# Two buffers of their own for the second weight quarter of a seven-product MLP round

## The chip, the cores and the metric

The kernel runs on one core of one Trainium2 chip. The metric is the time of one execution on the device in microseconds (us). TensorE (PE) multiplies, VectorE (DVE) and ScalarE (ACT) work on tiles, GpSimd (POOL) does small work and issues some transfers, and SyncE (SP) issues nearly all loads. A profile is one execution recorded by the hardware profiler. Its own time is its span, from the first to the last instruction.

## The reference, cut to what matters

Two token mixers (latent attention, then a Mamba-2 block) alternate with two dense MLPs, on 256 tokens of width 2048 in float32. The change lies in the MLP, which runs twice, with weights of 2048 x 8192 and 8192 x 2048:

```
def rms_norm(x, g):
    xf = x.astype(jnp.float32)
    y = xf * lax.rsqrt(jnp.mean(xf * xf, axis=-1, keepdims=True) + RMS_EPS)
    return (y * g.astype(jnp.float32)).astype(x.dtype)

def squared_relu_mlp(h, w_in, w_out):
    u = jax.nn.relu(h @ w_in)
    return (u * u) @ w_out

    for i in range(DEPTH):
        ...
        x = x + mix
        h = rms_norm(x, mlp_norm_g[i])
        x = x + squared_relu_mlp(h, mlp_w_in[i], mlp_w_out[i])
```

## The kernel before

**The stream of units.** All weights come as units of 128 x 1024 float32 (512 KB): two blocks of 128 rows of the contraction by 512 columns. `Flow` holds the list of units in the order in which PE uses them. Each unit is loaded by SP (line 85), then cut into a high and a low part so that three matmuls in PE's fast float32 format give nearly the full product: ACT writes the rounded high part `wh` (line 102), DVE subtracts it and writes the low part `wl` (line 103). The pools `wh` and `wl` have four buffers each. The pool of raw weights, `raw`, has six. The number in a tile's name is the number of its unit: `wl245` is the low part of unit 245.

**A round of seven products.** The first product of the MLP, 256 tokens by 2048 by 8192, runs in eight rounds p of 1024 hidden columns. Round 0 is computed in the plain way. Rounds 1 to 7 cut the tokens, the contraction and the columns into halves and use seven products of half-size blocks (M1, N7, N5, N6, N4, M2, N3) where eight would be needed. Each product runs in four steps d = 0 to 3 of two row blocks (six matmuls, lines 616 to 618). For a step four quarters of the weights are wanted: the first (b11) in pool `rx`, the second (b12), the fourth (b22), and the third for M2. DVE forms the combinations at line 183, in place:

```
if name == "N7":
    add("b22", "b12", "b22")
...
if name == "N5" and d not in LATE5:
    add("b12", "b11", "b12")
...
if name == "N6":
    add("b11", "b11", "b22")
    ...
"N7": lambda: [load("b12", B12, (0, 1)), load("b22", "raw", (1, 1))],
```

So the buffer of b12 is held from its load until the low part of N5 has been made from it, and the buffer of b22 from its load until the sum for N6 has read it. `LATE5` is empty.

**What sets the order.** `plan()` writes the order of PE's units by hand: products of round p are mixed with units `o` of the second product (w_out, `mo`) of the round before. PE's order is kept as written. The orders on SP, DVE, ACT and POOL are chosen when the program is built, by a scheduler that places each instruction where its own estimate sees it ready, so a new pool moves rows on these engines. On each engine the instructions run strictly in that order: SP holds back all loads behind one that still waits for a buffer.

**Units named below.** In the first MLP, round p = 4 has N7 of steps 0 to 3 as units 228, 234, 242 and 251; N6 of step 0 is unit 231, and units 246 and 247 belong to w_out. In round p = 7, N7 of steps 1 to 3 are units 368, 376 and 384.

Of the kernel before, what the change touches and what calls it, by code (L numbers as in the profile page):

```python
# [169 lines left out]
def seven(layer, p, src):  # L170
# [9 lines left out]
    def unit(flow, name, d):  # L180
# [22 lines left out]
        def load(k, pool, q):  # L203
            st[k] = Load(pool, quarter(d, *q))
            return st[k]

        loads = {"M1": lambda: [load("b11", "rx", (0, 0))],
                 "N7": lambda: [load("b12", B12, (0, 1)), load("b22", "raw", (1, 1))],
                 "M2": lambda: [load("M2", "raw", (1, 0))], "N3": lambda: [load("N3", "raw", (1, 1))]}
# [5 lines left out]
class Trunk:  # L215
# [294 lines left out]
    def mlp(self, layer, gain):  # L510
        with ExitStack() as ctx:
            mp = ctx.enter_context(self.tc.tile_pool(name="mlp", bufs=1, reuse_waits="tile"))
            for name, n in (("rx", 4), ("ry", 1)):
                self.flow.pools[name] = ctx.enter_context(self.tc.tile_pool(name=name, bufs=n, reuse_waits="tile"))
            self.flow.ahead = (4, 3)
            self.mlp_body(mp, layer, gain)
# [881 lines left out]
             "x7", "z5", "z6", "o2a", "z7", "o2b", "o3"]  # L1398


B12 = "raw"
WARM = 9
LATE5 = ()
TR = (10, 8, 7, 7, 5)
# [66 lines left out]
def sequence(d):  # L1471
# [23 lines left out]
    def mlp(i):  # L1495
# [9 lines left out]
        for nb in range(4):  # L1505
            for q in range(2):
                add(("mo", i, 7, nb, q), mo[14 + q, nb])

    mlp(0)
    col = lambda name, i: {"z": 0, "x": 8, "B": 16, "C": 18}[name] + i  # L1510
    si = lambda name, i: [add(("si", name, i, q), d["si"][q, col(name, i)]) for q in range(4)]
    so = lambda k, nb: add(("so", k, nb), d["so"][k, nb])
    for step in SSM_ORDER:
# [8 lines left out]
        else:  # L1522
            for pair in ((0, 1), (2, 3)):
                for k in (6, 7):
                    for nb in pair:
                        so(k, nb)
    mlp(1)
    return seq

# [78 lines left out]
```

## Time and profile before

| what | value |
|---|---|
| median of 3 runs (lowest to highest) | 2285.51 us (2285.43 to 2286.36) |
| span of the profiled execution | 2284.5 us |
| first MLP, about 271 to 925 us: PE, DVE, ACT busy | 653.83, 586.18, 414.11 us of 654.00 |
| second MLP, about 1606 to 2284.5 us: PE, DVE, ACT busy | 675.21, 594.88, 417.07 us of 678.50 |
| DMA moved in all | 557.16 MB, mean 244 GB/s |

The profiled execution has its span of 2284.5 us; the median of the timed runs lies 1.0 us above it. A matmul's end is modelled in the trace, so the distance from one matmul's start to the next tells of a wait, not its length. The rows of a timeline give the start, the duration, the engine, the line, the operation, what is written and read, and how many equal instructions are merged (x3: the duration runs from the first start to the last end).

### The profile page before, as it was taken

Reading aid. Unit: us, or ns where it says so; the run is one execution under the profiler, and the core shown is the slowest. Engines: PE = TensorE matmul, PEld = TensorE weight load, DVE = VectorE, ACT = ScalarE, POOL = GpSimd, SP = SyncE. Lnnn points to the kernel's source line nnn. Section 1 sums busy time; section 2 is a strip of 40 time slices with the busy share of each in tenths; the row PEclk is TensorE's granted clock in tenths of the full one; section 3 lists DMA queues with packets and bytes.
Section 4 is the critical chain, followed back from the end, with each engine's and each line's share of the span. In section 5 each row is a group of like instructions: output and inputs, shape, how many; then the busy total and the mean of one; then the engine's idle time right before and its main releaser. Section 6 shows DMA issues by size and latency. Waiting matters only on the chain.

```text
span 2284.5 us, 30768 instructions
## 1 busy us (share of the span) xinstructions
PE 2278.1 (100%) x10929; PEld 1889.6 (83%) x10929; DVE 1915.9 (84%) x2318; ACT 1390.1 (61%) x1947; POOL 275.5 (12%) x315
## 2 busy tenths in 40 slices
PE   9999999999999999999999999999999999999999
PEld 7898888888888888888888888888888888888887
DVE  7786698999898897687899688676989889989985
ACT  7775576566666666564666555545666666666663
POOL 1440000000000000100133213121000000000000
PEclk9999999999999999999999999999999999999999
DMA  8545678888888878667888787767688888888874
GB/s 315 173 153 159 211 230 267 259 255 270 264 255 259 267 232 271 227 208 241 277 280 278 245 275 264 229 222 229 204 265 248 259 270 253 260 275 247 267 232 160
DMA packets 167706, 557.16 MB, mean 244 GB/s; under 512 B 19040, under 2 KB 28192, under 8 KB 166528
## 3 DMA queue, kind: packets, MB, share of 16 engines
q1 hardware_dynamic: 151264, 502.44, 66.2%
q0 software_dynamic: 13888, 48.49, 10.0%
q10 hardware_dynamic: 2400, 4.27, 0.5%
q8 instruction: 86, 1.41, 0.3%
q14 instruction: 68, 0.56, 0.1%
HBM read 529.65 MB, written 6.41 MB: 235 GB/s over the span
## 4 chain that ended last, share of the span: by engine, by line
PE 96%; DVE 1%; DMA 1%; ACT 1%; issue 1%; POOL 0%; SPq 0%; ACTq 0%; DVEq 0%
PE acc L339 13%; PE acc L340 13%; PE acc L343 13%; PE yp L618 9%; PE yp L617 9%; PE yp L616 9%; PE st L617 7%; PE st L618 7%; PE st L616 7%; DMA wraw<-mi 1%; PE sm L324 1%; DVE wl L103 1%; PE y L1309 1%; PE sm L322 1%; PE acc L616 1%; PE acc L618 1%
## 5 line engine op out<-in xcount | busy, mean ns | idle before, releaser
L102 ACT ACTIVATE wh<-wraw 128x1024 fp32r<-128x1024 f32 (+1 forms) x818 | 856.2, 1053 | 570.4 <-PE acc L340 268.9
L103 DVE TENSOR_TENSOR wl<-wraw,wh 128x1024 fp32r<-128x1024 f32 (+1 forms) x818 | 985.5, 1221 | 240.6 <-ACT wh L102 216.6
L616 PE MATMUL yp<-wh,k 128*128 128x512 f32 x896 | 349.2, 390 | 0.0
L618 PE MATMUL yp<-wh,k 128*128 128x512 f32 x896 | 348.8, 389 | 0.0
L617 PE MATMUL yp<-wl,k 128*128 128x512 f32 x896 | 348.6, 389 | 0.0
L339 PE MATMUL acc<-wh,xt 128*128 128x512 f32 x704 | 279.7, 397 | 0.4 <-ACT wh L102 0.4
L340 PE MATMUL acc<-wh,xt 128*128 128x512 f32 x704 | 274.9, 390 | 0.1
L102 ACT ACTIVATE wh<-wrx 128x1024 fp32r<-128x1024 f32 x168 | 177.8, 1058 | 153.4 <-PE yp L618 101.7
L103 DVE TENSOR_TENSOR wl<-wrx,wh 128x1024 fp32r<-128x1024 f32 x168 | 204.3, 1221 | 36.6 <-ACT wh L102 35.6
L618 PEld LDWEIGHTS yp<-wh,k 128*128 128x128 f32 x896 | 168.2, 188 | 35.1
L617 PEld LDWEIGHTS yp<-wl,k 128*128 128x128 f32 x896 | 168.2, 188 | 34.9
L616 PEld LDWEIGHTS yp<-wh,k 128*128 128x128 f32 x896 | 168.2, 188 | 34.8
L339 PE MATMUL acc<-wh,k 128*128 128x512 f32 x496 | 196.5, 396 | 0.0
L340 PE MATMUL acc<-wh,k 128*128 128x512 f32 x496 | 193.3, 390 | 0.0
L343 PE MATMUL acc<-wl,xt 128*128 128x512 f32 x704 | 188.3, 389 | 0.0
L616 PE MATMUL st<-wh,xt 128*128 128x512 f32 x448 | 177.7, 397 | 0.0
L618 PE MATMUL st<-wh,xt 128*128 128x512 f32 x448 | 174.9, 390 | 0.0
L617 PE MATMUL st<-wl,xt 128*128 128x512 f32 x448 | 174.7, 390 | 0.0
L339 PEld LDWEIGHTS acc<-wh,xt 128*128 128x128 f32 x704 | 132.7, 188 | 29.4 <-ACT wh L102 1.6
L340 PEld LDWEIGHTS acc<-wh,xt 128*128 128x128 f32 x704 | 132.5, 188 | 28.5 <-issue 1.2
L343 PEld LDWEIGHTS acc<-wl,xt 128*128 128x128 f32 x704 | 132.1, 188 | 27.7
L199 POOL DMA_DIRECT2D wrx<-mi x56 | 49.2, 878 | 720.6 <-DVE wl L103 524.5
(318 smaller groups left out, 3527.0 us busy)
## 6 DMA issues: line engine op xcount, KB each, us to landing
wraw<-mi SPq DMA_DIRECT2D x256, 512.0 KB, 5.5
wraw<-mo SPq DMA_DIRECT2D x256, 512.0 KB, 5.6
wraw<-si SPq DMA_DIRECT2D x160, 512.0 KB, 5.2
wraw<-so SPq DMA_DIRECT2D x64, 512.0 KB, 5.2
wrx<-mi SPq DMA_DIRECT2D x56, 512.0 KB, 5.4
wrx<-mi POOLq DMA_DIRECT2D x56, 512.0 KB, 7.8
wraw<-wo SPq DMA_DIRECT2D x32, 512.0 KB, 4.0
taps<-xD SPq DMA_DIRECT2D x16, 768.0 KB, 8.4
```

What stands on the lines that cost most here:

```text
L102: self.last = nc.scalar.activation(h[:, v], raw[:, v], AF.Copy)
L103: self.last_lo = nc.vector.tensor_tensor(lo[:, v], raw[:, v], h[:, v].bitcast(F32), ALU.subtract)
L199: nc.gpsimd.dma_start(st["b11"].tile, quarter(d, 1, 0), accum_op=ALU.add)
L322: self.nc.tensor.transpose(b.bitcast(F32R)[:, v], words[:, v], self.ident_r)
L324: self.nc.tensor.transpose(b[:, v], src[:, v], self.ident)
L339: nc.tensor.matmul(accs[t][:, :n], ah, wh[:, q, :], start=first and kt + q == 0, stop=False)
L340: nc.tensor.matmul(accs[t][:, :n], al, wh[:, q, :], start=False, stop=False)
L343: nc.tensor.matmul(accs[t][:, :n], lhs(kt + q, t)[0], wl[:, q, :], start=False, stop=en and q == nk - 1)
L616: nc.tensor.matmul(b, ah, wh, start=first and q == 0, stop=False)
L617: nc.tensor.matmul(b, ah, wl, start=False, stop=False)
L618: nc.tensor.matmul(b, al, wh, start=False, stop=last and q == 1)
L1309: nc.tensor.matmul(y[t][c, o], part(t)[:, c], xg[g][t][:, o], start=True, stop=True)
```

## The change

```
-            for name, n in (("rx", 4), ("ry", 1)):
+            for name, n in (("rx", 4), ("ry", 1), ("rb", 2)):
                 self.flow.pools[name] = ctx.enter_context(self.tc.tile_pool(name=name, bufs=n, reuse_waits="tile"))
...
-B12 = "raw"
+B12 = "rb"
```

The MLP opens a pool `rb` of two buffers of 128 x 1024, and every second quarter (b12) of a round is loaded into it. The six `raw` buffers are left to the other weights. Each of 28 b12 loads per MLP moves the same bytes as before. PE's rows are the same and in the same order; rows on SP and DVE change place. Three places follow, with the buffer numbers kept; the last number in a name only tells tiles apart.

SP, at the start of round p = 4 of the first MLP, before (unit 224 ends round 3; 225, 226, 229, 232 and 235 belong to w_out; 228 and 234 are N7 of steps 0 and 1, each with two loads, b12 and b22):

```order
L85 DMA wraw224_5370<-mi0 128x1024
L85 DMA wrx250_5799<-mi0 128x1024
L85 DMA wraw225_5389<-mo0 128x1024
L85 DMA wraw226_5409<-mo0 128x1024
L85 DMA wraw228_5446<-mi0 128x1024
L85 DMA wraw228_5448<-mi0 128x1024
L85 DMA wraw229_5460<-mo0 128x1024
L85 DMA wraw232_5506<-mo0 128x1024
L85 DMA wraw234_5546<-mi0 128x1024
L85 DMA wraw234_5548<-mi0 128x1024
L85 DMA wraw235_5562<-mo0 128x1024
```

and now:

```order
L85 DMA wraw224_5373<-mi0 128x1024
L85 DMA wrx250_5802<-mi0 128x1024
L85 DMA wraw225_5392<-mo0 128x1024
L85 DMA wraw226_5412<-mo0 128x1024
L85 DMA wraw228_5451<-mi0 128x1024
L85 DMA wraw229_5463<-mo0 128x1024
L85 DMA wraw232_5509<-mo0 128x1024
L85 DMA wraw234_5551<-mi0 128x1024
L85 DMA wraw235_5565<-mo0 128x1024
```

The two b12 loads are gone from here (they stand many rows earlier as `wrb`). The b22 load of unit 234 now takes over the buffer of unit 224, where it took that of unit 226.

DVE, in the middle of the same round, before (`wraw251` are the two quarters of N7, step 3; x00 and x10 are the residual sums that free the two PSUM banks of pool `yp`):

```order
L103 TENSOR_TENSOR wl241_5715<-wrx241_5662,wh241_5714 128x1024
L183 TENSOR_TENSOR wrx241_5662<-wrx241_5662,wraw242_5682 128x1024
L103 TENSOR_TENSOR wl242_5733<-wraw242_5682,wh242_5732 128x1024
L103 TENSOR_TENSOR wl243_5745<-wraw243_5700,wh243_5744 128x1024
L103 TENSOR_TENSOR wl244_5758<-wraw242_5680,wh244_5757 128x1024
L103 TENSOR_TENSOR wl245_5771<-wrx241_5662,wh245_5770 128x1024
L103 TENSOR_TENSOR wl246_5782<-wraw246_5742,wh246_5781 128x1024
L436 TENSOR_TENSOR x00_142<-yp_544_5660,x00_142 128x512
L436 TENSOR_TENSOR x10_146<-yp_545_5661,x10_146 128x512
L183 TENSOR_TENSOR wraw251_5813<-wraw251_5811,wraw251_5813 128x1024
L103 TENSOR_TENSOR wl247_5802<-wraw247_5754,wh247_5801 128x1024
```

and now:

```order
L103 TENSOR_TENSOR wl241_5718<-wrx241_5665,wh241_5717 128x1024
L183 TENSOR_TENSOR wraw251_5816<-wrb251_5814,wraw251_5816 128x1024
L103 TENSOR_TENSOR wl242_5736<-wraw242_5685,wh242_5735 128x1024
L103 TENSOR_TENSOR wl243_5748<-wraw243_5703,wh243_5747 128x1024
L183 TENSOR_TENSOR wrx241_5665<-wrx241_5665,wraw242_5685 128x1024
L103 TENSOR_TENSOR wl244_5761<-wrb242_5683,wh244_5760 128x1024
L183 TENSOR_TENSOR wrb251_5814<-wrx250_5802,wrb251_5814 128x1024
L103 TENSOR_TENSOR wl245_5774<-wrx241_5665,wh245_5773 128x1024
L103 TENSOR_TENSOR wl246_5785<-wraw246_5745,wh246_5784 128x1024
L436 TENSOR_TENSOR x00_142<-yp_544_5663,x00_142 128x512
L436 TENSOR_TENSOR x10_146<-yp_545_5664,x10_146 128x512
L103 TENSOR_TENSOR wl247_5805<-wraw247_5757,wh247_5804 128x1024
```

The two sums of step 3 (line 183, unit 251) have moved ahead of the low parts of units 242 and 245 and of the residual sums. The same move is made in rounds 3 to 6 of both MLPs.

DVE, in the last round p = 7 of the first MLP, before:

```order
L103 TENSOR_TENSOR wl370_7792<-wraw368_7707,wh370_7791 128x1024
L103 TENSOR_TENSOR wl371_7810<-wraw371_7759,wh371_7809 128x1024
L183 TENSOR_TENSOR wraw376_7839<-wraw376_7837,wraw376_7839 128x1024
L103 TENSOR_TENSOR wl372_7822<-wrx359_7555,wh372_7821 128x1024
L183 TENSOR_TENSOR wraw376_7837<-wrx375_7819,wraw376_7837 128x1024
L103 TENSOR_TENSOR wl373_7843<-wrx365_7653,wh373_7842 128x1024
L103 TENSOR_TENSOR wl374_7856<-wraw374_7807,wh374_7855 128x1024
L436 TENSOR_TENSOR x00_142<-yp_637_7772,x00_142 128x512
L436 TENSOR_TENSOR x10_146<-yp_638_7773,x10_146 128x512
```

and now:

```order
L103 TENSOR_TENSOR wl370_7795<-wrb368_7710,wh370_7794 128x1024
L183 TENSOR_TENSOR wraw376_7842<-wrb376_7840,wraw376_7842 128x1024
L103 TENSOR_TENSOR wl371_7813<-wraw371_7762,wh371_7812 128x1024
L183 TENSOR_TENSOR wrb376_7840<-wrx375_7822,wrb376_7840 128x1024
L103 TENSOR_TENSOR wl372_7825<-wrx359_7558,wh372_7824 128x1024
L103 TENSOR_TENSOR wl373_7846<-wrx365_7656,wh373_7845 128x1024
L183 TENSOR_TENSOR wraw384_7961<-wrb384_7959,wraw384_7961 128x1024
L103 TENSOR_TENSOR wl374_7859<-wraw374_7810,wh374_7858 128x1024
L436 TENSOR_TENSOR x00_142<-yp_637_7775,x00_142 128x512
L436 TENSOR_TENSOR x10_146<-yp_638_7776,x10_146 128x512
```

Here too a sum of step 3 (unit 384) now stands ahead of the low part of unit 374 and of the residual sums, and the sum of step 2 (unit 376) ahead of the low part of unit 371.

## The prediction, made before the change was run

> **What bounds the kernel now.** I read the page's busy times first, then the waits by engine, then the stalls one by one in the timelines.
>
> ```profile
> PE 2278.1 (100%) x10929; PEld 1889.6 (83%) x10929; DVE 1915.9 (84%) x2318; ACT 1390.1 (61%) x1947; POOL 275.5 (12%) x315
> 271.00:925.00 654.00, 653.83 (x2961) 539.63 (x2959) 586.18 (x579) 414.11 (x452) 40.76 (x58) 1.00 0.83 256
> PE yp L939 <- ACT xt L944: 0.5, 1, 0.5
> PEld st L617 <- DVE wl L103: 3.2, 8, 0.5
> DVE wraw L183 <- DMA wraw<-mi: 18.1, 27, 2.0
> ```
>
> The second row is the stretch of the first MLP (length, then PE, PEld, DVE, ACT, POOL busy, clock, DMA share, GB/s): PE is busy in 653.83 of 654.00 us at the full granted clock. DVE is 90% busy behind it, so it has little to give. The largest wait of PE itself that is not at the kernel's start is 0.5 us, in attention. Of the weight loads ahead of PE, one wait belongs to the seven-product rounds: eight times, 3.2 us in all, for a low part from DVE. DVE's own wait for quarters (18.1 us) is far larger, but it costs only what reaches PE. So PE bounds the kernel, and a change in loads can give back little. That is the first thing to hold against any large gain.
>
> Where one of the eight waits comes from (round 4 of the first MLP, times from the span's start; DVE, then SP, then PE):
>
> ```profile
> 553.13 3.49 DVE L103 TENSOR_TENSOR wl<-wraw,wh 128x1024 fp32r<-128x1024 f32 x3
> 563.45 1.23 DVE L183 TENSOR_TENSOR wraw<-wraw,wraw 128x1024 f32<-128x1024 f32 x1 [0.54 <-DMA wraw<-mi]
> 566.33 1.22 DVE L183 TENSOR_TENSOR wrx<-wrx,wraw 128x1024 f32<-128x1024 f32 x1
> 568.73 1.23 DVE L103 TENSOR_TENSOR wl<-wrx,wh 128x1024 fp32r<-128x1024 f32 x1
> 555.51 1.47 SPq L85 DMA_DIRECT2D wraw<-mi  x2
> 569.55 0.40 PE L616 MATMUL st<-wh,sN 128*128 128x512 f32 x1
> 570.01 0.50 PE L617 MATMUL st<-wl,sN 128*128 128x512 f32 x1
> 570.35 0.40 PE L618 MATMUL st<-wh,sN 128*128 128x512 f32 x1
> 570.58 0.39 PE L616 MATMUL st<-wh,sN 128*128 128x512 f32 x1
> ```
>
> At 563.45 DVE stands 0.54 us for the quarters of unit 234 (N7, step 1). The sum for N6 of step 0 (566.33) and its low part (568.73) queue behind it, and PE, which wants that low part, starts its second matmul 0.46 us after the first and its third 0.34 us after that, where the step is 0.23 (570.35 to 570.58). That is 0.23 + 0.11 = 0.34 us lost. The two loads of unit 234 left SP only at 555.51 and 556.65, when the low parts of units 225 and 226 (second and third of the row at 553.13) had freed two of the six buffers.
>
> **The change part by part.** Counts do not change: as many loads, sums, splits and matmuls as before, so there is no work to add or take off. Only times of arrival move.
>
> (a) The stall above goes. The b12 load of unit 234 leaves this queue, and the b22 load takes the buffer of unit 224, freed when the first of the three low parts ends, at 553.13 + 1.22 = 554.35, instead of going out at 556.65. That is 2.3 us earlier for a wait of 0.54 us; the wait ends, unless `rb` itself is late. It is not: its buffer is released by the low part of N5 two steps back, more than 20 us before. Eight waits of 3.2 us in all, at the shown rate of 0.34 us of PE for a wait of 0.5: 3.2 x 0.34 / 0.5 = 2.2 us gained. Bounds: 0 and 3.2.
>
> The Trainium skill, Perfetto Trace Analysis, section Optimization Strategy, says that the same gap repeating on the engine that should be saturated can mean too little SBUF for the next tile, in the number of buffers. This trace agrees, with eight gaps of the same kind; by that rule alone the sum would be (a), and nothing would come back.
>
> (b) What is late next: the sums of step 3. In rounds 3 to 6 they now stand ahead of low parts that PE is about to want. The rows of before, DVE first, then the load queue, then PE:
>
> ```profile
> 584.88 2.35 DVE L103 TENSOR_TENSOR wl<-wrx,wh 128x1024 fp32r<-128x1024 f32 x2
> 588.41 3.49 DVE L103 TENSOR_TENSOR wl<-wraw,wh 128x1024 fp32r<-128x1024 f32 x3
> 594.50 1.28 DVE L436 TENSOR_TENSOR x<-yp,x 128x512 f32<-128x512 f32 x2
> 597.31 1.23 DVE L183 TENSOR_TENSOR wraw<-wraw,wraw 128x1024 f32<-128x1024 f32 x1 [1.53 <-DMA wraw<-mi]
> 578.09 3.70 SPq L85 DMA_DIRECT2D wraw<-mo  x4
> L183 DVE TENSOR_TENSOR wrx<-wrx,wraw x1: 1218/1218/1218, 580.2 to 580.2; 128x1024 f32<-128x1024 f32 x1
> DMA to landing us min/median/max: 4.3/6.4/6.6
> 590.92 0.39 PE L617 MATMUL st<-wl,sN 128*128 128x512 f32 x1
> 596.37 0.39 PE L617 MATMUL st<-wl,sN 128*128 128x512 f32 x1
> 597.50 0.39 PE L616 MATMUL yp<-wh,k 128*128 128x512 f32 x1
> ```
>
> The landing row is of the four loads that left from 578.09 on. The b22 of unit 251 now takes the buffer that the N6 sum of step 1 frees (580.2 + 1.22 = 581.4; 580.9 in the change, since DVE lost 0.54 us ahead of it). With the median landing of 6.4 us it is there at 587.3. DVE reaches the sum at 587.24 - 0.5 = 586.7 (end of the row at 584.88), stands 0.6 us, and starts it at 587.3. From there DVE is full, one operation per 1.135 us ((3.49 - 1.22) / 2): low part of 242 from 588.4 to 589.7, of 243 to 590.8, a sum, the low part of 244, another sum, the low part of 245 from 594.1 to 595.3, of 246 to 596.5, then the residual sums, the first until 597.1. PE, itself 0.34 us earlier, wants 242 at 590.6, 245 at 596.0 and, at 597.2, the bank that the first residual sum frees. So all is in time, by 0.1 us at the tightest place. At the longest landing of the four, 6.6, PE loses 0.1 us. At 4.3 there is a margin of 2.2. I take 0.1 us a round in 2 x 4 rounds, +0.8 us. Bounds: 0, and with 7.3 us, the longest landing of this pool near this place
>
> ```profile
> DMA to landing us min/median/max: 3.6/5.4/7.3
> ```
>
> (the loads from 552 to 572 us), 0.8 us a round, +6.4 us.
>
> (c) The last round. The sum of unit 384 stands ahead of the low part of 374 and the residual sums:
>
> ```profile
> 830.86 1.22 DVE L103 TENSOR_TENSOR wl<-wraw,wh 128x1024 fp32r<-128x1024 f32 x1
> 834.51 1.23 DVE L183 TENSOR_TENSOR wraw<-wraw,wraw 128x1024 f32<-128x1024 f32 x1 [0.81 <-DMA wraw<-mi]
> 839.06 1.22 DVE L103 TENSOR_TENSOR wl<-wraw,wh 128x1024 fp32r<-128x1024 f32 x1
> 840.19 1.28 DVE L436 TENSOR_TENSOR x<-yp,x 128x512 f32<-128x512 f32 x2
> DMA to landing us min/median/max: 4.5/6.7/7.0
> 842.01 0.39 PE L616 MATMUL yp<-wh,k 128*128 128x512 f32 x1
> ```
>
> After the low part of 370 (until 832.1) DVE now makes the sum of 376, whose wait of 0.81 us goes, and then the low part of 371, until 834.4; that frees the buffer for the b22 of 384. The four loads from 829.8 to 833.7 us took 4.5 to 7.0. From the sum's start it is 1.14 + 1.14 + 0.68 = 2.95 us to the end of the first residual sum, which PE wants at 842.0; the sum may start at 839.05 at the latest, so a landing up to 4.65 us costs nothing, and the median of 6.7 costs 2.05. I take 1.0 us, half of it, because the queue ahead of this load is shorter by one load and 0.7 us: +2.0 us for the two MLPs. Bounds: 0 and 4.7 (landing 7.0).
>
> The Trainium skill, SBUF — State Buffer, section The DMA setup-cost knee, gives a fit of 2 us plus bytes over 436 GB/s, an estimate of 3.2 us for a load of 512 KB. By it (b) and (c) would be nothing. The trace differs: no load in the three landing rows took less than 3.6 us, and the medians are 6.4, 5.4 and 6.7, so the measurement decides.
>
> (d) Costed at nothing. The first two b12 loads of each MLP now go out in attention and in the Mamba block, some 200 us and 50 us early, beside weights that PE needs there.
>
> ```profile
> q1 hardware_dynamic: 151264, 502.44, 66.2%
> 0.00:271.00 271.00, 268.03 (x1375) 230.39 (x1376) 195.63 (x432) 176.67 (x442) 67.97 (x117) 1.00 0.61 203
> ```
>
> 502.44 MB in 66.2% of the span is 332 GB/s, or 1.6 us a load. The DMA engines' share is 0.61 in the first stretch, so there is room; without that cover it would be at most 2 x 1.6 us per MLP. The new pool lies over memory that the Mamba block uses for tiles of its own; these are read long after the first MLP and given back before the second asks for it, so no wait follows. The two loads missing at the start of round 1 are a gain of the same size, not counted.
>
> Sum: -2.2 + 0.8 + 2.0 = +0.6 us on the profiled 2284.5, so 2285.1 for a span. The runs' median lies 1.0 us above the span: **2286.1 us**. What this kernel's measurement can tell from no change is about 0.2%, 4.6 us.
>
> **The rivals.**
>
> Slower: the sum of step 3 becomes the stall of every round. The place is the one of (b): a landing longer than 6.45 us goes to PE one for one, in eight rounds, and in (c) beyond 4.65 us, in two. It decides from about 6.8 us on, where 8 x 0.35 + 2 x 2.15 - 2.2 = +4.9 passes the 4.6. At 7.3 it is 8 x 0.85 + 2 x 2.65 - 2.2 = +9.9 us, 2296 us. For it: the last load of the burst is the slowest (6.6), and 27 waits of DVE for quarters show that this is where time runs short. Against it: the same burst with the same spacing gave 6.6 at most here. Chance 0.12.
>
> Faster by more than the bound: it would need 4.6 us, but all PE waits of this kind are 3.2 us, which gives 2282.3 us. The Trainium skill, Perfetto Trace Analysis, section Identifying the Most-Contended Engine, tells to judge TensorE by the share of its weight loads, and 83% would leave 17%. As a mechanism of this kernel, the idle part would have to be waiting for weights. It isn't: matmul follows matmul at 0.23 us wherever the operands are there (570.35 to 570.58). Chance 0.02.
>
> The change does not do what it says: the new order of SP brings the b22 of unit 234 no earlier, the eight waits stay, and (b) and (c) come on top or not: 2285.5 to 2288.3 us. Against it is the buffer of unit 224, freed 2.3 us earlier. Part of the case of no change, 0.08 of its chance.
>
> **How the numbers follow.** The forecast, stalls taken away in one place and given back in another, within 0.2% of 2285.5: 0.86 with the last rival. Slower 0.12, faster 0.02. The range goes from 2283.6 (1.9 of the 2.2 of (a), and nothing of (b) and (c)) to 2290.6 (2285.5 + 5.1, just beyond the landing of 6.8 us at which the slower rival begins to decide), which leaves out most of that rival.
>
> **What would show it.** Right: no wait of PE's weight loads for `wl` of N6, step 0 (unit 231 and its like in rounds 3 to 6); DVE's total wait for quarters of pool `raw` well below 18.1 us; a DVE wait of 0.3 to 1 us ahead of the sum of unit 251, on one load, and about 1 us lost by PE ahead of the first matmul of unit 374. Wrong: PE starts more than 0.5 us apart around units 242, 245 or 246 in each round; a stall in attention or the Mamba block that was not there; or MLP rounds that are shorter by more than 0.4 us each.

## The result, and the profile after

The changed kernel takes 2289.73 us (median of 19 runs, 2287.84 to 2291.73), the kernel before 2286.22 us (median of 19 runs, 2285.22 to 2287.26). The ratio is 1.0015, with a 95% interval of 1.0008 to 1.0022: slower by 3.5 us. That lies inside the range of the forecast (2283.6 to 2290.6) and below the 0.2% that was put as the bound of no change, but it is no zero, and the forecast's own +0.6 us is too small. The profiled executions differ by a little less, 2287.3 against 2284.5 us, so the traces account for 2.8 of the 3.5 us.

The page's busy times and the waits by engine of the changed kernel (of a wait, behind the colon: total us, times, longest):

```profile
PE 2279.1 (100%) x10929; PEld 1888.9 (83%) x10929; DVE 1914.5 (84%) x2318; ACT 1388.8 (61%) x1947; POOL 276.2 (12%) x315
DVE wraw L183 <- DMA wraw<-mi: 11.3, 12, 1.3
PE yp L616 <- DVE x L436: 2.3, 6, 0.4
PEld st L617 <- DVE wl L103: 1.7, 7, 0.3
PEld yp L616 <- ACT wh L102: 5.2, 8, 0.8
```

The second row is shorter than before (it was 18.1 us in 27 waits). The third row is new: PE itself now waits, six times, for a residual sum that frees a PSUM bank. Of the fourth row's kind there were eight waits with 3.2 us before. Six of these eight were at N6 of step 0, and those are gone; the two others, at 882 and 2216 us before, 0.3 us each, are still there, and the five new ones stand in the middle of rounds. The fifth row is new too, and it is the largest, but it shows the same stops as the third: it is the weight load of the matmul that waits for the bank (two of the eight are too short for the third row).

Round 4 of the first MLP in the changed kernel, at the two places of the prediction (timeline; PE at N6 of step 0, then SP, DVE, ACT, PE and its weight load in the middle of the round):

```profile
569.58 0.40 PE L616 MATMUL st<-wh,sN 128*128 128x512 f32 x1
569.82 0.39 PE L617 MATMUL st<-wl,sN 128*128 128x512 f32 x1
570.04 0.40 PE L618 MATMUL st<-wh,sN 128*128 128x512 f32 x1
578.59 0.33 SPq L85 DMA_DIRECT2D wrb<-mi  x1
579.73 0.33 SPq L85 DMA_DIRECT2D wraw<-mo  x1
580.86 0.33 SPq L85 DMA_DIRECT2D wraw<-mi  x1
582.06 0.33 SPq L85 DMA_DIRECT2D wrx<-mi  x1
584.35 2.35 DVE L103 TENSOR_TENSOR wl<-wrx,wh 128x1024 fp32r<-128x1024 f32 x2
587.90 1.23 DVE L183 TENSOR_TENSOR wraw<-wrb,wraw 128x1024 f32<-128x1024 f32 x1 [1.19 <-DMA wraw<-mi]
589.04 2.35 DVE L103 TENSOR_TENSOR wl<-wraw,wh 128x1024 fp32r<-128x1024 f32 x2
596.99 1.28 DVE L436 TENSOR_TENSOR x<-yp,x 128x512 f32<-128x512 f32 x2
596.03 1.06 ACT L102 ACTIVATE wh<-wraw 128x1024 fp32r<-128x1024 f32 x1 [0.25 <-PE st L618]
597.02 0.39 PE L618 MATMUL st<-wh,sN 128*128 128x512 f32 x1
597.78 0.19 PEld L616 LDWEIGHTS yp<-wh,k 128*128 128x128 f32 x1 [0.80 <-ACT wh L102]
597.82 0.47 PE L616 MATMUL yp<-wh,k 128*128 128x512 f32 x1 [0.40 <-DVE x L436]
```

At N6 the matmuls follow each other at 0.22 to 0.24 us: the stall is gone. In the middle of the round DVE stands 1.19 us for the b22 of unit 251 (issued at 580.86). From then on it works without a break, and its first residual sum starts at 596.99, 9.09 us after the late sum started. PE has finished unit 245 by then and starts unit 246 at 597.82, 0.80 us after its last matmul, where 0.23 is the step: 0.57 us lost, and 0.12 us more in single steps beside the gap. ACT had written the high part of unit 246 by 597.09, in time, though the profile names it for the wait of the weight load. What came last is the residual sum: at each of the eight stops PE starts 0.15 us after the first residual sum ends (597.67 here). The landing of that load, from the rows of its tile:

```profile
DMA to landing us min/median/max: 6.9/6.9/6.9
```

Between the two traces the same matmul can be compared: at N6 PE is 0.31 us ahead of the kernel before (570.04 against 570.35), at the first matmul of unit 246 it is 0.32 us behind (597.82 against 597.50). Done so over the whole program, this gives the account below.

| where | PE, us |
|---|---|
| kernel's first 13 us | -0.2 |
| five of the six stalls at N6, step 0 (the sixth had cost PE nothing) | -1.7 |
| middle of rounds 3 to 6, both MLPs: 0.2, 0.7, 0.8, 0.0, then 0.8, 0.6, 0.6, 0.7 | +4.4 |
| last round, both MLPs | +0.2 |
| all (with 0.1 in round 2; the parts are rounded) | +2.8 |

### The profile page after: what moved, and what is told of

Its sections match the earlier page's. It is cut to its first block, busy times and chain, and to the rows that moved or that the text cites. A ratio compares the mean times of both kernels' runs of the same rounds, so it can differ in the third digit from the quotient of the medians.

```text
span 2287.3 us, 30747 instructions
## 1 busy us (share of the span) xinstructions
PE 2279.1 (100%) x10929; PEld 1888.9 (83%) x10929; DVE 1914.5 (84%) x2318; ACT 1388.8 (61%) x1947; POOL 276.2 (12%) x315
## 4 chain that ended last, share of the span: by engine, by line
PE 93%; DVE 3%; DMA 1%; issue 1%; ACT 1%; POOL 0%; SPq 0%; ACTq 0%; DVEq 0%
PE acc L339 13%; PE acc L340 13%; PE acc L343 13%; PE yp L616 9%; PE yp L618 9%; PE yp L617 9%; PE st L618 7%; PE st L616 7%; PE st L617 7%; DVE wl L103 2%; PE sm L324 1%; PE y L1309 1%; PE sm L322 1%; PE acc L616 1%; PE acc L617 1%
## 5 line engine op out<-in xcount | busy, mean ns | idle before, releaser
L102 ACT ACTIVATE wh<-wraw 128x1024 fp32r<-128x1024 f32 (+2 forms) x762 | 797.4, 1052 | 536.3 <-PE acc L340 274.4
L103 DVE TENSOR_TENSOR wl<-wraw,wh 128x1024 fp32r<-128x1024 f32 (+2 forms) x762 | 920.1, 1221 | 238.0 <-ACT wh L102 222.7
L103 DVE TENSOR_TENSOR wl<-wrx,wh 128x1024 fp32r<-128x1024 f32 x168 | 204.4, 1221 | 49.2 <-ACT wh L102 48.3
```

What stands on the lines that cost most here:

```text
L102: self.last = nc.scalar.activation(h[:, v], raw[:, v], AF.Copy)
L103: self.last_lo = nc.vector.tensor_tensor(lo[:, v], raw[:, v], h[:, v].bitcast(F32), ALU.subtract)
```

## The experiments

Three theories stood against each other. **Q**: the step-3 sum stands at the head of DVE's queue until its b22 lands; what the landing takes beyond some 6.3 us reaches PE. **T**: the loads, now in another order, make weights late wherever DVE takes them. **P**: two buffers for b12 are too few. The expectations speak of the gap "at unit 247"; it stands ahead of the first matmul of unit 246, as shown above.

**Only DVE's order put back.** Loads, buffers and the orders of SP, ACT and POOL are those of the changed kernel. `issue_after(x)` keeps an instruction behind x in the order of its engine; `last_x` is the last residual sum.

```
-                add("b22", "b12", "b22")
+                with flow.tc.issue_after(flow.last_x.ins) if d == 3 and p > 1 else ExitStack(): add("b22", "b12", "b22")
...
```

> The changed kernel, with one thing put back: on DVE the sum of N7, step 3, of each round from 2 on is queued behind the residual sums, as in the kernel before; every load and every other engine keeps the order of the changed kernel. Theory Q (the step-3 sum stands at the head of DVE's queue until its b22 quarter lands, and the low parts and residual sums behind it reach PE late): the gaps of 0.46 to 0.59 us ahead of the first matmul of unit 247 are gone, and the eight stalls at N6, step 0, stay gone, so 1.5 to 2.2 us below the kernel before, about 2284.4 us against 2286.2, ratio 0.9990 to 0.9995. Theory T (the loads themselves are what slows it: they go out in another order, more of them at once, and weights come late wherever DVE takes them): as the changed kernel, +3 to +4 us, ratio 1.0015.

Measured: 2284.35 us (2284.06 to 2284.78) against 2286.29, ratio 0.9992, interval 0.9983 to 1.0001. Waits and timeline of this run (round 5 of the first MLP), and the landing of its b22, which left at 664.0:

```profile
DVE wraw L183 <- DMA wraw<-mi: 0.2, 1, 0.2
677.34 1.28 DVE L436 TENSOR_TENSOR x<-yp,x 128x512 f32<-128x512 f32 x2
678.53 1.22 DVE L183 TENSOR_TENSOR wraw<-wrb,wraw 128x1024 f32<-128x1024 f32 x1
680.11 0.39 PE L618 MATMUL st<-wh,sN 128*128 128x512 f32 x1
680.34 0.39 PE L616 MATMUL yp<-wh,k 128*128 128x512 f32 x1
DMA to landing us min/median/max: 7.7/7.7/7.7
```

The quarter took 7.7 us, longer than in the changed kernel's round 4, and PE lost nothing (680.11 to 680.34): the sum now stands behind the residual sums (678.53 after 677.34). All eight middles are free of loss, and the five stalls at N6 stay gone. T falls. The cause of the slowdown is one move in DVE's order that the build-time scheduler made when the pool was added. (With this sum two others of line 183 change place on DVE: the second sum of step 3, which needs it, and an N6 sum, which comes forward. The burst run below leaves DVE's order alone and shows that it is the wait for the load that costs.)

**Three buffers for b12.**

```
-            for name, n in (("rx", 4), ("ry", 1), ("rb", 2)):
+            for name, n in (("rx", 4), ("ry", 1), ("rb", 3)):
...
-        self.st = pool("stat", 24)
+        self.st = pool("stat", 12)
```

The pool of small statistics tiles gives the room; no row on DVE, ACT or POOL changes place.

> The changed kernel with three buffers in the own pool of b12 where it has two (to make room, the pool of small statistics tiles has 12 where it had 24). The b12 of step 3 goes out one buffer earlier; DVE's order is that of the changed kernel. Theory Q: the b22 quarter is what the sum waits for, and it takes its buffer and its place as in the changed kernel, so the time stays +3 to +4 us, ratio 1.0013 to 1.0018. Theory P (two buffers are too few: the b12 of step 3, issued only when the low part of N5, step 1, has been made, is what comes late): the gaps at unit 247 go, 1.5 to 2.2 us below the kernel before, ratio 0.9993.

Measured: 2289.51 us (2287.34 to 2291.75), ratio 1.0014 (1.0005 to 1.0023). Nothing is won by a third buffer while the sum stands early: P falls for two buffers. The b12 of step 3 now lands some 10 us before its b22 leaves, but the first b12 of the next round has taken its place in the burst (below).

**The other quarter in the own pool.**

```
-        "N7": lambda: [load("b12", B12, (0, 1)), load("b22", "raw", (1, 1))],
+        "N7": lambda: [load("b12", "raw", (0, 1)), load("b22", B12, (1, 1))],
```

> The two quarters change places: b22 has the pool of two buffers, b12 goes back to the six. DVE's order is that of the changed kernel, with the step-3 sum early. Theory Q: the b22 of step 3 now waits for the N6 sum of step 1 in its own pool, which ends when it did, so its issue and its landing are the same: the gaps at unit 247 stay, +3 to +4 us, ratio 1.0015. Theory P, or any theory by which it matters which quarter holds the own pool: another time, in either direction by 2 us or more.

Measured: 2291.08 us (2288.2 to 2292.41), ratio 1.0019 (1.001 to 1.0028). The gaps stay, as Q has it; 0.85 us come on top in the last round of the first MLP, where the b12, now in the six, lands last.

**A load of 256 KB more ahead of the late quarter.**

```
+            with self.tc.issue_after(self.last_load.ins) if getattr(ld, "late", 0) else ExitStack(): self.nc.sync.dma_start(self.pools["more"].tile([P, 512], F32, tag="more", name=f"more{self.loaded}"), ld.src[:, 512:]) if getattr(ld, "late", 0) else None
             self.last_load = self.nc.sync.dma_start(ld.tile[:, o:z], ld.src[:, o:z])
...
```

> The changed kernel with one more load of 256 KB on SP just ahead of the b22 load of step 3, in rounds 3 to 6 of both MLPs, into a tile that nobody reads. At the rate of 332 GB/s it takes 0.8 us of the DMA engines. DVE's order is that of the changed kernel. Theory Q: the b22 lands up to 0.8 us later, 7.2 to 7.8 us after its issue where 6.1 to 7.1 were measured, and all of it beyond 6.4 us goes to PE in each of eight rounds: 8 x (0.8 to 1.4), so 6 to 11 us above the kernel before, ratio 1.0027 to 1.0048. Theories T and P: 2 MB more in 557 MB, +0 to +1 us over the changed kernel, ratio 1.0015 to 1.0019.

Measured: 2301.52 us (2300.44 to 2302.05), ratio 1.0066 (1.0054 to 1.0079). That is 15 us over the kernel before, on the side of Q but beyond its 6 to 11. The worst place, round 5 of the first MLP (timeline and tile rows of this run):

```profile
677.57 1.22 DVE L183 TENSOR_TENSOR wraw<-wrb,wraw 128x1024 f32<-128x1024 f32 x1 [3.91 <-DMA wraw<-mi]
677.35 0.39 PE L616 MATMUL st<-wh,sN 128*128 128x512 f32 x1
679.98 0.78 PE L617 MATMUL st<-wl,sN 128*128 128x512 f32 x1 [2.25 <-DVE wl L103]
DMA to landing us min/median/max: 9.7/9.7/9.7
```

The eight landings have a median of 8.3 us, where the changed kernel has 6.9: a load that is worth 0.8 us of the DMA engines delayed the quarter behind it by 1.4. PE stands here at the low part of unit 286 (the like of 242), which waits behind the sum. In the four other rounds with a landing beyond 8 us it stands there and then once more at the bank; here the matmuls behind the stall run slowly, and the residual sums are in time (last section).

In the first four kernels with the early sum, the loss of a round can be set against the landing. Some of the 32 rounds, from the traces (issue to landing of the b22 of step 3; loss of PE in the 19 us after the issue, against the same matmuls in the kernel before):

| kernel, round of the first MLP | landing, us | PE lost, us | landing - 6.25 |
|---|---|---|---|
| changed, 6 | 6.1 | 0.0 | below 0 |
| changed, 3 | 6.4 | 0.2 | 0.2 |
| changed, 4 | 6.9 | 0.7 | 0.7 |
| 256 KB more, 4 | 7.4 | 1.1 | 1.1 |
| three buffers, 5 | 8.2 | 1.9 | 2.0 |
| 256 KB more, 3 | 8.8 | 2.5 | 2.5 |
| sum held back, 5 | 7.7 | 0.0 | 1.4 |

With the early sum each microsecond beyond 6.25 is one of PE (more in the one round whose clock fell, last section); with the sum held back none is.

**The burst thinned.** From the run with three own buffers on, the next round's first b12 goes out behind the b22. DVE's order is the slow one.

```
+            with self.tc.issue_after(self.b22_3.ins) if getattr(ld, "late", 0) and hasattr(self, "b22_3") else ExitStack(): self.last_load = self.nc.sync.dma_start(ld.tile[:, o:z], ld.src[:, o:z]); self.b22_3 = self.last_load if getattr(ld, "third", 0) else getattr(self, "b22_3", self.last_load)
+            st[k] = Load(pool, quarter(d, *q)); st[k].late = (k, d) == ("b12", 0) and p > 3; st[k].third = (k, d) == ("b22", 3)
```

> The run with three own buffers, with one load moved on SP: the first b12 of the next round, which stood two loads ahead of the b22 of step 3, now goes out behind it (rounds 4 to 7 of both MLPs). DVE's order stays that of the changed kernel, with the step-3 sum early. In the four runs so far PE lost what the b22 took beyond 6.25 us from issue to landing. Theory Q with bursts (the landing is long because four loads go out within 3.5 us and share the DMA engines): 512 KB less ahead of it, at 332 GB/s 1.6 us less, so 4.6 to 6.6 us to landing where 6.2 to 8.2 were measured, and no more than 0.35 us lost in a round: 2284.4 to 2286 us, ratio 0.9990 to 1.0000, though the order on DVE is that of the slower kernel. Theory L (the landing has another cause than the loads just ahead, such as where in memory the quarter lies): as with three own buffers, 2289.5 us, ratio 1.0014.

Measured: 2284.93 us (2284.17 to 2287.5), ratio 0.9993 (0.9985 to 1.0002). Round 5 of the first MLP with three own buffers (SP's and DVE's timeline):

```profile
661.82 0.68 SPq L85 DMA_DIRECT2D wrb<-mi  x1
662.96 0.33 SPq L85 DMA_DIRECT2D wraw<-mo  x1
664.09 0.33 SPq L85 DMA_DIRECT2D wraw<-mi  x1
672.33 1.23 DVE L183 TENSOR_TENSOR wraw<-wrb,wraw 128x1024 f32<-128x1024 f32 x1 [2.41 <-DMA wraw<-mi]
```

and the same place with the burst thinned:

```profile
662.69 0.33 SPq L85 DMA_DIRECT2D wraw<-mo  x1
663.83 0.33 SPq L85 DMA_DIRECT2D wraw<-mi  x1
665.02 0.33 SPq L85 DMA_DIRECT2D wrx<-mi  x1
665.40 0.42 SPq L85 DMA_DIRECT2D wrb<-mi  x1
669.89 1.23 DVE L183 TENSOR_TENSOR wraw<-wrb,wraw 128x1024 f32<-128x1024 f32 x1 [0.23 <-DMA wraw<-mi]
DMA to landing us min/median/max: 6.0/6.0/6.0
```

The `wrb` load stands behind the b22 (665.40 after 663.83), the quarter lands after 6.0 us where it took 8.2, and DVE waits 0.23 us for it instead of 2.41. Over the eight rounds the median goes from 7.0 to 5.8 us, 1.2 us for 512 KB, less than the 1.6 expected, and PE loses 0.1 us in all. L falls as the main cause: the loads just ahead make the landing long. What L has left is that round 5 of the first MLP lands late in the changed kernel and in the first four runs (7.1, 8.2, 8.5, 9.7, 7.7 us). But the kernel that took 7.7 us there took 6.9 in its second profile (last run below), and 7.4 in round 3: the landing of one and the same load changes from one execution to the next, and why round 5 is often the late one stays open.

**One own buffer, and five raw buffers, both with the sum held back.**

```
-            for name, n in (("rx", 4), ("ry", 1), ("rb", 2)):
+            for name, n in (("rx", 4), ("ry", 1), ("rb", 1)):
```

> The run with the step-3 sum held behind the residual sums, with one buffer for b12 where it has two. A b12 can go out only when the low part of N5 of the step before has been made, and SP holds back what stands behind it. Theory Q: what counts is that no sum whose quarter is still on its way stands ahead of low parts that PE wants, and that the b22 of step 1 finds a free buffer earlier than in the kernel before; one own buffer gives both, so 2284.4 to 2285.2 us, ratio 0.9991 to 0.9996. Theory P (it takes two buffers): the b12 becomes the late quarter, at the sums of steps 1 and 2, and the eight stalls at N6, step 0, come back or grow: 2286 us and more.

Measured: 2331.42 us (2327.4 to 2331.63), ratio 1.019 (1.0176 to 1.0204). Q's numbers were far off here, P is right for one buffer. Its waits:

```profile
DVE wraw L183 <- DMA wrb<-mi: 60.4, 30, 4.1
PE st L617 <- DVE wl L103: 16.8, 25, 1.8
PE yp L616 <- DVE x L436: 6.7, 18, 0.4
```

DVE waits 60 us for b12 quarters, up to 4.1 us at a time, and PE waits for low parts in rounds 1 to 6 of both MLPs. DVE's order differs here in other places too, so the 45 us aren't split between the late b12 and that order.

```
-        self.wp = {"raw": pool("raw", 6), "wh": pool("wh", 4), "wl": pool("wl", 4)}
+        self.wp = {"raw": pool("raw", 5), "wh": pool("wh", 4), "wl": pool("wl", 4)}
```

> The run with the step-3 sum held behind the residual sums, with five buffers for raw weights where it has six (seven in all where the kernel before had six). The b22 of step 1 takes a buffer that comes free 1.1 us later than in the held run, still 1.1 us before that of the kernel before, where it was 0.54 us late; the b22 of step 3 goes out later too, but its sum stands later. Theory Q: no stall in the MLP, 2284.4 to 2285 us, ratio 0.9991 to 0.9995. Theory R (six raw buffers are needed, in attention and the Mamba block above all, whose weights have no other pool): over 2288 us, with the loss outside the MLP.

Measured: 2291.73 us (2289.74 to 2293.99), ratio 1.0023 (1.0014 to 1.0032). Its waits:

```profile
PEld acc L343 <- DVE wl L103: 4.2, 3, 2.6
PE acc L343 <- DVE wl L103: 2.9, 3, 2.2
```

Line 343 is in the Mamba block: there PE lost 4.5 us between 1221 and 1274 us, while the MLPs kept 1.0 us of what they gained (a stall at N6 is back in the second MLP). The profiled execution is the fastest of the eleven, so the trace accounts for 3.4 of the 5.2 us. R is right: the six serve more than the MLP, and the own pool can't be paid for with one of them.

**Both remedies together, and the held sum once more.**

> Both remedies together: three own buffers with the next round's first b12 behind the b22 of step 3 on SP, and the step-3 sum held behind the residual sums on DVE. Theory Q with bursts: each of the two alone took away nearly all that PE lost in the middle of the rounds, and they work on the same wait, so together they give what one gives: 2284.3 to 2284.9 us, ratio 0.9990 to 0.9994. Theory 2 (they are two separate losses): another 1 us or more below, under 2283.5 us.

Measured: 2284.30 us (2284.05 to 2284.92), ratio 0.9991 (0.9982 to 1.0). One remedy is as good as both: they act on one wait. The thinned burst shortens the landing here too, from a median of 6.9 us (the sum held back alone) to 6.1.

> The run with the step-3 sum held behind the residual sums, once more, to narrow its interval: theory Q 2284.4 us, ratio 0.9992 (0.9988 to 0.9996 with the eight stalls' 1.7 us of the trace). If the first run's gain was chance: 2286.3 us, ratio 1.0000.

Measured: 2284.37 us (2283.89 to 2285.48), ratio 0.9991 (0.9982 to 1.0). The version with two own buffers and the sum held back lies about 2 us below the kernel before, in both its runs, and its traces are 1.7 and 1.8 us shorter, nearly all of it at just the five stalls at N6. The intervals reach to 1.0, so the gain is read from the traces, not proved by the times.

## Why the prediction was right or wrong

**What bounds the kernel**: right. PE is the path in each kernel, and every change in time is found again in the distances between its matmuls.

**(a) The stall at N6**: right in kind. All are gone, in every kernel with six raw buffers and an own pool of two or more. The term was -2.2; it measured -1.7. The row of 3.2 us was read as eight stalls at N6 of step 0, but only six waits with 2.6 us are there (rounds 4 and 6 of the first MLP, 3 to 6 of the second), and one of 0.2 us had cost PE nothing. The two others, 0.3 us each, stay in the changed kernel and with the sum held back.

**(b) The sums of step 3**: the mechanism, its place and the order of events were right: issue at 580.9 (580.86 measured), then DVE full to the residual sum, then PE at the bank. The size was wrong: +0.8 was put, +4.4 measured. The step that failed is the one that sets landing and slack against each other, "all is in time, by 0.1 us at the tightest place". The landing was 6.9 us (median of eight), not the 6.4 taken from four `mo` loads of another burst; and the slack ends at 6.25 us, not 6.45. Costed at nothing were the hand-overs, from the landing to DVE (0.02 to 0.12 us) and from DVE's sum to PE (597.67, the end of the first of the two sums at 596.99, to 597.82), and the 0.12 us lost in steps beside the gap. Together these are somewhat more than 0.2 us; a few hundredths in the forecast's chain take the rest back. With 6.9 the forecast's own rule gives 0.45 us a round and 3.6 us in all. Behind it stands a sentence of (a): that the b12's buffer is released 20 us early is right for step 1, whose b12 is the only one that it looked at, but the b12 of step 3 takes the buffer that N5 of step 1 frees, and goes out at 578.59, two loads ahead of the b22, into the same burst. The thinned burst shows what that costs.

**(c) The last round**: +2.0 was put, +0.2 measured. The changed kernel's rows there:

```profile
831.97 0.33 SPq L85 DMA_DIRECT2D wrb<-mi  x1
834.58 0.33 SPq L85 DMA_DIRECT2D wraw<-mi  x1
839.61 1.23 DVE L183 TENSOR_TENSOR wraw<-wrb,wraw 128x1024 f32<-128x1024 f32 x1 [0.98 <-DMA wraw<-mi]
841.89 1.28 DVE L436 TENSOR_TENSOR x<-yp,x 128x512 f32<-128x512 f32 x2
842.63 0.39 PE L618 MATMUL st<-wh,sN 128*128 128x512 f32 x1
842.86 0.39 PE L616 MATMUL yp<-wh,k 128*128 128x512 f32 x1
DMA to landing us min/median/max: 4.9/4.9/4.9
```

DVE does wait, 0.98 us, but this load leaves 2.6 us after the one ahead of it and lands in 4.9 us, and PE starts at 842.86 without a gap. The landing was taken from bursts (median 6.7); this load, further behind the one ahead, is faster, and its like in the second MLP takes 5.1 us. So (b) and (c) failed on one number, in opposite directions: a landing time of another place was used without looking at what leaves SP within some 3 us ahead of the load.

**(d) The early loads in attention and in the Mamba block**: right. The same matmuls run within 0.2 us of their old distance from 13 to 450 us and from 900 to 1606 us.

**The rivals.** The slower one named the true mechanism, and that the landing goes to PE one for one is what the table of landings shows; it put its threshold 0.2 us too high and, with (c) at nothing, it fell 1 us short of the bound at which it was to decide. The forecast's case of no change won by that alone. That the time fell inside the range is luck in part: against the trace (a) was 0.5 us too hopeful, (b) 3.6 us too low and (c) 1.8 us too high. With (c) as forecast the time would have been some 2291.5 us, outside. Two figures of the rival and of (b) are also off by their own rule: 2285.5 + 9.9 is 2295.4 us, not 2296, and 7.3 us of landing is 0.85 us a round, 6.8 in all, not 6.4. "The change doesn't do what it says" is out.

**The signs to look for.** No wait for low parts at N6 of step 0 and a DVE wait for raw quarters well below 18.1 us (11.3) came as named. A DVE wait of 0.3 to 1 us ahead of the sum of unit 251 was named as right; it is 1.19. PE starts more than 0.5 us apart around unit 246 were named as wrong, and are there in six of the eight rounds. Of the 1 us ahead of unit 374 nothing came.

## What to carry to other kernels

Where a scheduler orders the engines, a new buffer moves work as well as loads: look in the new order for an operation that waits for a transfer and now stands ahead of operations that need nothing, and hold it back. Take a load's landing time from a load that leaves into the same burst, not from the median of its kind, leave room for its change from one execution to the next (7.7 and 6.9 us for one load of one kernel), and add the hand-over at both ends when a margin is only a few tenths. A pool's size has to be checked against the step that releases its buffers for each user of it: here one buffer cost 45 us, two gained 2 us with the sum held back, and three gained nothing more.

## What the runs showed that was not expected

A wait of PE can cost more than its length. In round 5 of the run with 256 KB more, PE stood 2.25 us, and the next eight matmuls ran at half speed (windows of that run: PE, PEld, DVE, ACT, POOL busy, granted clock, DMA share, GB/s):

```profile
680.00:683.00 3.00, 3.00 (x7) 2.44 (x8) 3.00 (x3) 0.69 (x1) 0.00 (x0) 0.51 0.29 53
683.50:686.00 2.50, 2.50 (x13) 2.06 (x11) 2.50 (x3) 1.03 (x2) 0.02 (x1) 1.00 0.96 290
```

The granted clock is 0.51 for some 3.5 us and then 1.00 again; at 0.20 us a matmul that is some 1.6 us lost beside the stall. The residual sums had that time to be ready, so the stall at the bank did not come, and the round lost 4.1 us where 9.65 - 6.25 = 3.4 would have been its share. A wait of 2.16 us in the run with five raw buffers left the clock at full speed:

```profile
1261.14 1.21 PE L343 MATMUL acc<-wl,k 128*128 128x512 f32 x4 [2.16 <-DVE wl L103]
```

The Trainium skill, TensorE: Matmul & The Clock Gate, section HAM oscillation — how this bites in real kernels, puts the rule as no idle gaps of PE over about 3.4 us. The trace differs: 2.25 us was enough here, once; with one case on either side, whether length or phase decides stays open.

The second is how a burst shares the engines: 256 KB more ahead of a load delayed it by 1.4 us and 512 KB less brought it 1.2 us forward (0.8 with the sum held back), where the mean rate of 332 GB/s gives 0.8 and 1.6.
